# RWKV-7 layer on one core: the recurrence's products and outputs issued in pairs on opposite column tiles, its state sums in pairs with U

## The chip, the core and the metric

The kernel runs on one core of a Trainium2 chip. The metric is the device time in microseconds (us) of one execution. Three runs of the kernel before took 1661.93, 1671.85 and 1673.42 us, so the median is 1671.85. The profiled execution took 1675.05 us, of which 1673.2 us are the span from its first to its last instruction.

The engines are PE (TensorE: matrix products; PEld is its weight load), DVE (VectorE), ACT (ScalarE), POOL (GpSimd) and SP (SyncE, which here only issues DMAs). Each engine runs its own instructions in the order in which they are written, and waits on semaphores for the others.

## The reference

Only layer 0 of the trunk is computed (depth 1), for 2048 tokens, width 1024, 16 heads of 64: an RMS norm, a token shift, projections to r, k, v, gate, decay and a per-channel rate a, a recurrence per head, a group norm, a bonus, a gate and an output projection.

```
dx = token_shift(h) - h;  x_i = h + dx * mu[i]
r, k, v = x_r @ w_r, x_k @ w_k, x_v @ w_v;  g = silu(x_g @ w_g)
decay, a from two small low-rank products;  kk = normalized k * k_k
step(S):  sa = S @ -kk_t
          S = S * decay_t + sa (kk_t * a_t)' + v_t k_t'
          y_t = S @ r_t
y = groupnorm(y) + (r . k . r_k) v;  out = x + (y * g) @ w_out
```

## The kernel before, in words

The program has three stages. Stage one makes the norm, the shifted inputs, and the projections v and gate. Stage two makes, for eight blocks of 256 tokens, the projections k and r and from them the small matrices of the recurrence, which it writes to DRAM; its last block runs the first nine chunks of the recurrence between the pieces of its own work. Stage three runs the other 55 chunks and the output projection. The change touches the last block of stage two and all of stage three.

The recurrence is done in 64 chunks of 32 tokens. A chunk `ch` has two half-steps, `w` = 0 and 1, one for each half of the 16 heads (four pairs `p`, two heads `h` each). A half-step consists of four sets of small float32 products on PE. Each product has 32 output columns and goes to one of four column tiles of 32 (`tile_position`), at 0, 32, 64 or 96:

- **S** (`s_mm`, L255): the products of the chunk's matrix with the state and the values; 8 products, on two column tiles, to `bank[w]`. ACT copies the result (`s_out`, L261) into `misc` or `aux`.
- **U** (`u_mm`, L267): the inverse applied to that copy; 8 products, on two column tiles, to `bank[2]`. ACT copies it into the chunk's `x` (`u_out`, L273).
- **Y** (`y_mm`, L279): the output of the chunk; 8 products, on two column tiles; ACT copies them to `y` on odd chunks (`y_out`, L292).
- **D** (`d_mm`, L300 in the kernel before): the sums for the state; 16 products, on all four column tiles, to `bank[3]`. DVE multiplies them with the decay into the next chunk's `x` (`d_out`, two instructions that the profile has at L52, x<-ubank).

`bank[2]` and `bank[3]` are the two halves of one tile, `ubank` (in stage two `ud`). For one `w`, the chain S, s_out, U, u_out, D, d_out leads from one chunk to the next; the two values of `w` alternate, so Y and D of a half-step belong to the other `w`, half a chunk earlier.

Between these sets the kernel calls `fill`. In stage three `fill` is `after(i)`: first `background(BG)` takes pieces of the group norm, bonus and gating of finished tiles of 128 tokens (`tail`: y instructions on DVE, squares on ACT, a Newton chain on POOL at L405 and L406, transposes on PE at L446) from a list, up to a budget of estimated us per call; a piece `(None, None)` ends a call. Then `fill(F[i % 2])` takes up to that many matmuls of 128x512 of the output projection (`mm`, L486, called dense here) from another list. The amount is multiplied by 1.3, 1 or 0.7, by how many are waiting. The list `work` also takes the columns of a triangular inversion (`inversion`, tiles z and tm on DVE) for two later blocks. PE, DVE, ACT and POOL keep the written order exactly (`manual_schedule`).

Of the kernel before, what the change touches and what calls it, by code (L numbers as in the profile page):

```python
# [24 lines left out]
L = 32  # L25
TB = 256
NC = TB // L
NORM_EPS = 1e-6
F, BG, EV, EV0, GWE, BNE, LOW, SLOW, FAST, INV, INVC = (2, 4), 1.3, (0, 0, 0), (0, 0, 0), 0, 0, 36, 0.7, 1.3, (8, 10), 0.5
LIM = 1.0  # L30
TURN = 1e-9
INL = (0, 0, 3, 3, 3, 0, 0, 0)
# [8 lines left out]
def rwkv7_kernel(ctx, tc, a, T):  # L41
# [209 lines left out]
    def s_mm(ch, w, p):  # L251

        for h in range(2):
            o = col(h, ch + w)
            nc.tensor.matmul(bank[w][o, 1, p], stat[ch % len(stat)][:, h, 4 * w + p, ca], xs[ch % len(xs)][:, h, 4 * w + p],  # L255
                             start=True, stop=True, tile_position=(0, o.start))

    def s_out(ch, w):
        with urgent():
            for h in range(2):  # L260
                nc.scalar.copy(live(w, h)[bu(h)], bank[w][col(h, ch + w), 1])  # L261

    def u_mm(ch, w, p):

        for h in range(2):
            o = col(h, ch)
            nc.tensor.matmul(bank[2][o, p], stat[ch % len(stat)][:, h, 4 * w + p, ca], live(w, h)[:, p], start=True, stop=True,  # L267
                             tile_position=(0, o.start))
# [22 lines left out]
            elif c % 2:  # L291
                nc.scalar.copy(ys[t][:, c // 2, 4 * w : 4 * w + 4], bank[w][:, 0])  # L292

    def d_mm(ch, w):
        if ch + 1 < NCH:
            d, x = dk[ch % len(dk)], xs[ch % len(xs)]
            for p in range(4):
                for h in range(2):
                    for o in (64 * (1 - h), 64 * (1 - h) + L):
                        nc.tensor.matmul(bank[3][o : o + L, p], d[:, h, 4 * w + p, o % 64 : o % 64 + L], x[:, h, 4 * w + p],  # L300
                                         start=True, stop=True, tile_position=(0, o))

    def d_out(ch, w):

# [8 lines left out]
    def chunk(ch, fill):  # L313

        g, c = divmod(ch, NC)
        go = ch != first[0]
        if c == 2 and g + 1 < NB:
            load_g(g + 1)
        for w in range(2):
            for p in range(4):  # L320
                s_mm(ch, w, p)
            s_out(ch, w)
            if w or go:
                end(ch - 1 + w, 1 - w)
            if w == 0:
                if ch + 2 < NCH:
                    load_v(ch + 2)
                if ch + 3 < NCH:
                    load_c(ch + 3)
            fill(2 * w)  # L330
            for p in range(4):
                u_mm(ch, w, p)
            u_out(ch, w)
            fill(2 * w + 1)

    def end(ch, w):

        d_mm(ch, w)
        d_out(ch, w)
        for p in range(4):  # L340
            y_mm(ch, w, p)
        y_out(ch, w)

    dense, evacs, turned, served, al, parts_of = deque(), deque(), set(), [0.0, 0.0], {"low": LOW}, {}
    eng = lambda i: nc.gpsimd if i else nc.vector

    def fill(n):

        served[0] = min(served[0], 6) + n * (FAST if len(dense) > 2 * al["low"] else 1 if len(dense) > al["low"] else SLOW)
        while served[0] > 0 and dense:  # L350
            dense.popleft()[0]()
            served[0] -= 1
# [5 lines left out]
    def tail(t, ks=(0, 1)):  # L358
# [140 lines left out]
        if len(ks) == 1:  # L499
            k = ks[0]  # L500
            out.extend(parts[2 * k] + parts[2 * k + 1] + [(None, None), (0, lambda: (transpose(k), high(k))), (0.7, lambda: rest(k))])
            if k == 0:
                return out, []
            cut = 0
        elif t == 0:

            turns = [[(TURN, lambda k=k: (transpose(k), high(k), rest(k)))] for k in range(2)]
            cut = len(out)
            out.extend(parts[0] + parts[1] + turns[0] + parts[2] + parts[3] + turns[1])
        else:  # L510

            turns = [[(None, None), (0, lambda k=k: (transpose(k), high(k)))] for k in range(2)]
            rests = [[(0.7, lambda k=k: rest(k))] for k in range(2)]
            out.extend(parts[0] + parts[1] + parts[2] + turns[0] + parts[3] + rests[0])
            cut = len(out)
            out.extend([(None, None), (0.0, lambda: None)] + turns[1] + rests[1])
        out.append((0.0, lambda: dense.extend((lambda n=n, ct=ct, k=k: mm(n, ct, k), t)
                                              for n in range(2) for ct in range(NCT) for k in range(3))))
        return out[:cut], out[cut:]
# [697 lines left out]
    with ExitStack() as p1:  # L1217
        def pool(n, bufs, **k):
            return p1.enter_context(tc.tile_pool(name=n, bufs=bufs, reuse_waits="tile", **k))

        c1, yp = pool("c1", 1), pool("yp", 1)
        sps, tps = pool("sps", 1, space=PSUM), pool("tps", 2, space=PSUM)
        for w in range(2):
            bank[w] = sps.tile([P, 2, 4, N], F32, name=f"ybank{w}")
        ud = sps.tile([P, 2, 4, N], F32, name="ubank")
        bank[2], bank[3] = ud[:, 0], ud[:, 1]
        work = deque()
        evs[:] = EV
        al.update(rs=nc.gpsimd, newton=0, wait=2)
        al["sml"] = lambda nm: yp.tile([P, 2, NP], F32, name=nm, tag="sml", bufs=8)  # L1230
        al["sq"] = lambda nm: yp.tile([P, 4, N], F32, name=nm, tag="big", bufs=4)
        al["v"] = lambda nm: yp.tile([P, NP, N], F32, name=nm, tag="v", bufs=4)
        al["o"] = lambda nm: yp.tile([P, NCT, P], F32R, name=nm, tag=nm[:2], bufs=2)
        al["yt"] = lambda nm: tps.tile([P, 4, P], F32, name=nm, tag="tps")
        al["gt"] = lambda nm: yp.tile([P, NP, N], F32, name=nm, tag="gt", bufs=2)
        gb1 = c1.tile([P, 2, 4, N], F32, name="gb")
        nc.sync.dma_start(gb1, a["gn_b"].rearrange("p (i h n) -> p i h n", i=2, n=N))
        al["gb"] = lambda i: gb1[:, i]

        def background(us):  # L1240

            served[1] = min(served[1] + us, us)
            fresh = True
            while evacs or work:
                u, fn = (evacs or work)[0]
                if not fresh and (u is None or u > served[1]):
                    break
                (evacs or work).popleft()
                if u is None:
                    continue  # L1250
                fresh = False
                fn()
                served[1] -= u

        def more_y(t):
            while t > 5 and t - 3 not in turned:
                background(1)
            return yp.tile([P, 2, NP, N], F32, name=f"y{t}", tag="y", bufs=3)

        more[0], first[0] = more_y, NC + 1  # L1260

        with tc.manual_schedule(engines=MANUAL):
            work.extend((0.7, lambda q=q: wo_split(NP - 1, q)) for q in range(2))
            for x in tail(1):
                work.extend(x)
            z = c1.tile([P, L, L], F32, name="z_")
            tm = c1.tile([P, 4 * N], F32, name="tm_")
            inv = deque()
            for g in (NB - 2, NB - 1):
                load, *cols = inversion(g, z, lambda: tm)  # L1270
                inv.extend([(0, load)] + [(None, None), (0, lambda: None)] * 4)
                inv.extend((INVC, x) for x in cols)
            inv_g = inv[L + 6][1]

            inv_last = inv[-1][1]

            def after(i):
                background(BG)
                fill(F[i % 2])

            for ch in range(NC + 1, NCH):
                chunk(ch, after)
                if ch % 4 == 0 and ch > NC:
                    for x in tail(ch // 4 - 1):
                        work.extend(x)
                    for i in range(INV[1] if ch >= INV[0] else 0):
                        if inv:
                            work.append(inv.popleft())
                if ch == NCH - 8:

                    al["low"] = 0
                if ch == NCH - 2:

                    al.update(rs=nc.vector, newton=0.8, wait=0)
                    work.extend(tail(NCH // 4 - 1, (0,))[0])
                if ch == NCH - 2 * NC - 4:
                    assert len(inv) <= L - 1 and not any(x[1] is inv_g for x in work)
                if ch == NCH - NC - 4:
                    assert not inv and not any(x[1] is inv_last for x in work)
            end(NCH - 1, 1)  # L1300
            work.extend(tail(NCH // 4 - 1, (1,))[1])
            while work or dense or evacs:
                background(2)
                fill(6)
# [53 lines left out]
```

## Time and profile before

| | us |
|---|---|
| median of three runs | 1671.85 |
| profiled execution, its own time | 1675.05 |
| its span | 1673.2 |
| stages one and two (0 to 1149) | 1149 |
| stage three, while chunks run (1149 to 1606) | 457 |
| stage three, after the last chunk (1606 to 1673) | 67 |

The profile is of one execution. A group of rows gives an engine, a line of the kernel, an operation, the tiles written and read, and a shape. An idle time is put down to what ended it. The small products of the recurrence are pipelined: a row "x28, 0.58 us" means that 28 of them started and that the last one ended 0.58 us after the first start. A float32 product is two instructions.

### The profile page before, as it was taken

Reading aid. Unit: us, or ns where it says so; the run is one execution under the profiler, and the core shown is the slowest. Engines: PE = TensorE matmul, PEld = TensorE weight load, DVE = VectorE, ACT = ScalarE, POOL = GpSimd, SP = SyncE. Lnnn points to the kernel's source line nnn. Section 1 sums busy time; section 2 is a strip of 40 time slices with the busy share of each in tenths; the row PEclk is TensorE's granted clock in tenths of the full one; section 3 lists DMA queues with packets and bytes.
Section 4 is the critical chain, followed back from the end, with each engine's and each line's share of the span. In section 5 each row is a group of like instructions: output and inputs, shape, how many; then the busy total and the mean of one; then the engine's idle time right before and its main releaser. Section 6 shows DMA issues by size and latency. Waiting matters only on the chain. (4 is left out here: it accounts for less than half of the span.)

```text
span 1673.2 us, 48351 instructions
## 1 busy us (share of the span) xinstructions
PE 1523.3 (91%) x19024; PEld 1257.4 (75%) x19024; DVE 1193.8 (71%) x2917; ACT 762.1 (46%) x1908; POOL 352.8 (21%) x703
## 2 busy tenths in 40 slices
PE   3799999999989999999999997978999998899986
PEld 2578888888878898888888886766666666666765
DVE  7987688676744687979797886666656767766574
ACT  5653233323564545455455544655444444444420
POOL 4500000000012323232222324112222222232220
PEclk9899999999999999999999998989999999999998
DMA  5773334235653556666656578777756577566631
GB/s 180 229 255 140 130 134 147 98 131 170 210 171 87 150 117 156 150 147 165 153 156 149 144 159 213 188 209 190 217 169 176 169 169 194 163 169 181 172 96 47
DMA packets 413409, 269.78 MB, mean 161 GB/s; under 512 B 270048, under 2 KB 345440, under 8 KB 413184
## 3 DMA queue, kind: packets, MB, share of 16 engines
q1 hardware_dynamic: 411840, 262.19, 56.5%
q10 hardware_dynamic: 1344, 4.52, 1.1%
q8 instruction: 150, 2.46, 0.6%
q14 instruction: 75, 0.61, 0.1%
HBM read 159.26 MB, written 111.54 MB: 162 GB/s over the span
## 5 line engine op out<-in xcount | busy, mean ns | idle before, releaser
L52 DVE TENSOR_TENSOR x<-ubank,misc 64x256 f32<-64x256 f32 x216 | 91.1, 422 | 125.2 <-PE ubank L300 121.9
L575 PE MATMUL kps<-mixbl,wkh 128*128 128x256 f32 x448 | 131.7, 294 | 14.8 <-DVE mixbl L187 14.8
L273 ACT COPY x<-ubank 32x256 f32<-32x256 f32 x220 | 79.9, 363 | 128.2 <-PE ubank L267 82.2
L223 POOL MEMSET x<- 32x512 f32 x128 | 66.3, 518 | 328.3 <-PE ybank L279 264.2
L575 PE MATMUL kps<-mixbh,wkh 128*128 128x256 f32 x448 | 135.3, 302 | 0.0
L883 PE MATMUL rps<-mixah,wrh 128*128 128x256 f32 x448 | 133.0, 297 | 2.1 <-ACT sq L61 2.1
L575 PE MATMUL kps<-mixbh,wkl 128*128 128x256 f32 x448 | 130.7, 292 | 0.0
L883 PE MATMUL rps<-mixal,wrh 128*128 128x256 f32 x448 | 127.3, 284 | 0.0
L883 PE MATMUL rps<-mixah,wrl 128*128 128x256 f32 x448 | 127.2, 284 | 0.0
L486 PE MATMUL ops<-woh,oh 128*128 128x512 f32 x256 | 111.6, 436 | 2.4 <-ACT oh L466 2.0
L486 PE MATMUL ops<-woh,ol 128*128 128x512 f32 x256 | 113.3, 443 | 0.0
L486 PE MATMUL ops<-wol,oh 128*128 128x512 f32 x256 | 110.5, 432 | 0.0
L575 PE MATMUL vps<-wvh,mixah 128*128 128x512 f32 x256 | 104.3, 409 | 5.9 <-ACT mixah L97 5.4
L61 ACT ACTIVATE th<-wa,dprm 128x256 f32<-128x256 f32 x64 | 30.3, 474 | 161.1 <-PE wa L835 92.8
L575 PEld LDWEIGHTS kps<-mixbl,wkh 128*128 128x128 f32 x448 | 89.9, 201 | 16.0 <-DVE mixbl L187 16.0
L575 PE MATMUL vps<-wvl,mixah 128*128 128x512 f32 x256 | 101.9, 399 | 0.0
L575 PE MATMUL gps<-wgh,mixbh 128*128 128x512 f32 x256 | 99.9, 390 | 0.0
L575 PE MATMUL gps<-wgl,mixbh 128*128 128x512 f32 x256 | 99.8, 390 | 0.0
L575 PE MATMUL gps<-wgh,mixbl 128*128 128x512 f32 x256 | 99.8, 390 | 0.0
L575 PEld LDWEIGHTS kps<-mixbh,wkh 128*128 128x128 f32 x448 | 89.6, 200 | 9.0 <-issue 9.0
L883 PEld LDWEIGHTS rps<-mixah,wrh 128*128 128x128 f32 x448 | 85.9, 192 | 12.8 <-issue 8.6
L873 POOL TENSOR_TENSOR ra<-th,e 128x256 f32<-128x256 f32 x56 | 47.3, 844 | 218.5 <-issue 149.9
(341 smaller groups left out, 4408.8 us busy)
## 6 DMA issues: line engine op xcount, KB each, us to landing
stat<-sm_d SPq DMA_DIRECT2D x64, 512.0 KB, 4.9
dk<-bt_d SPq DMA_DIRECT2D x128, 128.0 KB, 4.5
sm_d<-ra SPq DMA_DIRECT2D x112, 128.0 KB, 2.6
sm_d<-mo SPq DMA_DIRECT2D x112, 128.0 KB, 2.9
bt_d<-bo SPq DMA_DIRECT2D x56, 256.0 KB, 2.9
up<-up_d SPq DMA_DIRECT2D x66, 128.0 KB, 2.7
xn<-x SPq DMA_DIRECT2D x32, 256.0 KB, 5.2
mkr_d<-mok SPq DMA_DIRECT2D x64, 128.0 KB, 1.7
```

What stands on the lines that cost most here:

```text
L52: return nc.vector.tensor_tensor(out=out, in0=in0, in1=in1, op=op)
L61: nc.scalar.activation(out, in_, f, **k)
L223: nc.gpsimd.memset(x[bu(h), h], 0.0)
L273: (nc.vector.tensor_copy if w and h and evs[0] else nc.scalar.copy)(xs[ch % len(xs)][bu(h), h, 4 * w : 4 * w + 4], bank[2][col(h, ch)])
L486: nc.tensor.matmul(ps, l[:, ct], r(ct, ns), start=(ct == 0 and k == 0), stop=(ct == NCT - 1 and k == 2))
L575: nc.tensor.matmul(ps, x, y, start=first, stop=last)
L873: (nc.vector if b == NB - 1 else nc.gpsimd).tensor_tensor(out=ra[:, :, ca], in0=c3(kn), in1=e[:, :, 0:L], op=mul)
L883: nc.tensor.matmul(ps, x, y, start=first, stop=last)
```

## The change

In a half-step S and Y are now issued in turn, pair by pair, and Y's column tiles are the two that S doesn't use. D and U are issued in turn as well, after three dense matmuls (before: D came straight after S, and U after Y and two dense ones). `F` goes from (2, 4) to (3, 3), the budget `BG` from 1.3 to 1.7 and, in the last four chunks, to 2.4. A forced pause before the second transposes of a tile is taken out, and the inversion's columns join the list in two lots of five in place of one of ten. The first output of stage three has no predecessor as before (`go`).

```diff
--- before.py
+++ after.py
@@ -26,7 +26,7 @@
 TB = 256
 NC = TB // L
 NORM_EPS = 1e-6
-F, BG, EV, EV0, GWE, BNE, LOW, SLOW, FAST, INV, INVC = (2, 4), 1.3, (0, 0, 0), (0, 0, 0), 0, 0, 36, 0.7, 1.3, (8, 10), 0.5
+F, BG, EV, EV0, GWE, BNE, LOW, SLOW, FAST, INV, INVC = (3, 3), (1.7, 2.4), (0, 0, 0), (0, 0, 0), 0, 0, 36, 0.7, 1.3, (8, 10), 0.5
 LIM = 1.0
 TURN = 1e-9
 INL = (0, 0, 3, 3, 3, 0, 0, 0)
@@ -291,14 +291,13 @@
             elif c % 2:
                 nc.scalar.copy(ys[t][:, c // 2, 4 * w : 4 * w + 4], bank[w][:, 0])
 
-    def d_mm(ch, w):
+    def d_mm(ch, w, p):
         if ch + 1 < NCH:
             d, x = dk[ch % len(dk)], xs[ch % len(xs)]
-            for p in range(4):
-                for h in range(2):
-                    for o in (64 * (1 - h), 64 * (1 - h) + L):
-                        nc.tensor.matmul(bank[3][o : o + L, p], d[:, h, 4 * w + p, o % 64 : o % 64 + L], x[:, h, 4 * w + p],
-                                         start=True, stop=True, tile_position=(0, o))
+            for h in range(2):
+                for o in (64 * (1 - h), 64 * (1 - h) + L):
+                    nc.tensor.matmul(bank[3][o : o + L, p], d[:, h, 4 * w + p, o % 64 : o % 64 + L], x[:, h, 4 * w + p],
+                                     start=True, stop=True, tile_position=(0, o))
 
     def d_out(ch, w):
 
@@ -313,33 +312,40 @@
     def chunk(ch, fill):
 
         g, c = divmod(ch, NC)
-        go = ch != first[0]
+        go = ch > max(first[0], 0)
         if c == 2 and g + 1 < NB:
             load_g(g + 1)
         for w in range(2):
+            old = (ch - 1 + w, 1 - w) if w or go else None
             for p in range(4):
                 s_mm(ch, w, p)
+                if old:
+                    y_mm(*old, p)
             s_out(ch, w)
-            if w or go:
-                end(ch - 1 + w, 1 - w)
+            if old:
+                y_out(*old)
+            fill(2 * w)
+            for p in range(4):
+                if old:
+                    d_mm(*old, p)
+                u_mm(ch, w, p)
+            if old:
+                d_out(*old)
+            u_out(ch, w)
             if w == 0:
                 if ch + 2 < NCH:
                     load_v(ch + 2)
                 if ch + 3 < NCH:
                     load_c(ch + 3)
-            fill(2 * w)
-            for p in range(4):
-                u_mm(ch, w, p)
-            u_out(ch, w)
             fill(2 * w + 1)
 
     def end(ch, w):
-
-        d_mm(ch, w)
-        d_out(ch, w)
         for p in range(4):
             y_mm(ch, w, p)
         y_out(ch, w)
+        for p in range(4):
+            d_mm(ch, w, p)
+        d_out(ch, w)
 
     dense, evacs, turned, served, al, parts_of = deque(), deque(), set(), [0.0, 0.0], {"low": LOW}, {}
     eng = lambda i: nc.gpsimd if i else nc.vector
@@ -513,7 +519,7 @@
             rests = [[(0.7, lambda k=k: rest(k))] for k in range(2)]
             out.extend(parts[0] + parts[1] + parts[2] + turns[0] + parts[3] + rests[0])
             cut = len(out)
-            out.extend([(None, None), (0.0, lambda: None)] + turns[1] + rests[1])
+            out.extend(turns[1] + rests[1])
         out.append((0.0, lambda: dense.extend((lambda n=n, ct=ct, k=k: mm(n, ct, k), t)
                                               for n in range(2) for ct in range(NCT) for k in range(3))))
         return out[:cut], out[cut:]
@@ -1275,20 +1281,22 @@
             inv_last = inv[-1][1]
 
             def after(i):
-                background(BG)
+                background(BG[first[0] < 0])
                 fill(F[i % 2])
 
             for ch in range(NC + 1, NCH):
                 chunk(ch, after)
                 if ch % 4 == 0 and ch > NC:
+
                     for x in tail(ch // 4 - 1):
                         work.extend(x)
-                    for i in range(INV[1] if ch >= INV[0] else 0):
-                        if inv:
-                            work.append(inv.popleft())
+                        work.extend(inv.popleft() for i in range(min(len(inv), INV[1] // 2) if ch >= INV[0] else 0))
                 if ch == NCH - 8:
 
                     al["low"] = 0
+                if ch == NCH - 4:
+
+                    first[0] = -1
                 if ch == NCH - 2:
 
                     al.update(rs=nc.vector, newton=0.8, wait=0)
```

**PE, stage three, one half-step and the next.** Before (tile names as the program has them; ubank holds D at L300 and U at L267, ybank S at L255 and Y at L279, ops the dense matmuls):

```order
L255 MATMUL ybank_14828<-x_12870,stat_12863 32x64 x8
L300 MATMUL ubank<-x_12872,dk_12866 32x64 x16
L279 MATMUL ybank_14829<-x_12872,stat_12862 32x64 x8
L486 MATMUL ops_21207<-woh_14283,oh_20878 128x512
L486 MATMUL ops_21207<-wol_14284,oh_20878 128x512
L267 MATMUL ubank<-misc,stat_12863 32x64 x8
L486 MATMUL ops_21207<-woh_14283,ol_20879 128x512
L486 MATMUL ops_21207<-woh_14492,oh_20878 128x512
L486 MATMUL ops_21207<-wol_14493,oh_20878 128x512
L486 MATMUL ops_21207<-woh_14492,ol_20879 128x512
L486 MATMUL ops_21207<-woh_14675,oh_20878 128x512
L486 MATMUL ops_21207<-wol_14676,oh_20878 128x512
```

After (Y is still L279, D is L299, the dense matmuls are L492); the cut begins with the second half of a set of S and Y:

```order
L255 MATMUL ybank_14829<-x_12872,stat_12862 32x64 x2
L279 MATMUL ybank_14828<-x_12872,stat_12862 32x64 x2
L255 MATMUL ybank_14829<-x_12872,stat_12862 32x64 x2
L279 MATMUL ybank_14828<-x_12872,stat_12862 32x64 x2
L492 MATMUL ops_21467<-woh_13457,oh_20779 128x512
L492 MATMUL ops_21467<-wol_13458,oh_20779 128x512
L492 MATMUL ops_21467<-woh_13457,ol_20780 128x512
L299 MATMUL ubank<-x_12872,dk_12866 32x64 x4
L267 MATMUL ubank<-aux,stat_12862 32x64 x2
L299 MATMUL ubank<-x_12872,dk_12866 32x64 x4
L267 MATMUL ubank<-aux,stat_12862 32x64 x2
L299 MATMUL ubank<-x_12872,dk_12866 32x64 x4
```

S and Y alternate by two; three dense matmuls follow; then D and U alternate by four and two. U no longer stands behind Y and two dense matmuls alone, and D no longer ahead of them.

**DVE, stage three, between the start of the Newton chain (written to g) and the first y that reads its end (rst).** x<-ubank,misc x2 is d_out. Before:

```order
L401 TENSOR_REDUCE var_0_20478<-sq_3_20506 128x4
L52 TENSOR_TENSOR x_12870<-ubank,misc 64x256 x2
L58 TENSOR_SCALAR var_0_20478<-var_0_20478 128x16
L58 TENSOR_SCALAR g_0_20557<-var_0_20478 128x16
L52 TENSOR_TENSOR x_12871<-ubank,misc 64x256 x2
L49 SCALAR_TENSOR_TENSOR xr_20339<-ops_20338,xr_20339 128x256
L49 SCALAR_TENSOR_TENSOR xr_20341<-ops_20338,xr_20341 128x256
L52 TENSOR_TENSOR x_12871<-ubank,misc 64x256 x2
L52 TENSOR_TENSOR y_19209<-y_19209,rst_0_20479 128x256
```

After:

```order
L52 TENSOR_TENSOR x_12871<-ubank,misc 64x256 x2
L407 TENSOR_REDUCE var_0_22112<-sq_3_22128 128x4
L58 TENSOR_SCALAR var_0_22112<-var_0_22112 128x16
L58 TENSOR_SCALAR g_0_22172<-var_0_22112 128x16
L52 TENSOR_TENSOR x_12872<-ubank,misc 64x256 x2
L52 TENSOR_TENSOR y_21645<-y_21645,rst_0_22113 128x256
```

Two d_out pairs stood between g and the y instruction, and one stands there now.

**PE, the end of the program: the transposes of the last tile of tokens (yt) and what stands around them.** Before:

```order
L486 MATMUL ops_22579<-woh_14675,oh_22495 128x512
L486 MATMUL ops_22579<-wol_14676,oh_22495 128x512
L486 MATMUL ops_22579<-woh_14675,ol_22496 128x512
L446 MATMUL yt_22626<-consts,y_22030 128x128 x4
L446 MATMUL yt_22675<-consts,y_22030 128x128 x4
L486 MATMUL ops_22682<-woh_13272,oh_22624 128x512
L486 MATMUL ops_22682<-wol_13273,oh_22624 128x512
```

After, where the first set of that tile (yt_22611) is the first row, and that of its second half comes right below the last:

```order
L452 MATMUL yt_22611<-consts,y_22213 128x128 x4
L492 MATMUL ops_22587<-wol_14044,oh_22408 128x512
L492 MATMUL ops_22587<-woh_14043,ol_22409 128x512
L492 MATMUL ops_22587<-woh_14258,oh_22408 128x512
L492 MATMUL ops_22587<-wol_14259,oh_22408 128x512
L492 MATMUL ops_22587<-woh_14258,ol_22409 128x512
L492 MATMUL ops_22587<-woh_14467,oh_22408 128x512
L492 MATMUL ops_22587<-wol_14468,oh_22408 128x512
L492 MATMUL ops_22587<-woh_14467,ol_22409 128x512
L492 MATMUL ops_22587<-woh_14650,oh_22408 128x512
L492 MATMUL ops_22587<-wol_14651,oh_22408 128x512
L492 MATMUL ops_22587<-woh_14650,ol_22409 128x512
```

Both sets stood behind all 48 dense matmuls of the tile ahead; now the first set stands eleven dense matmuls earlier. Over the whole program the dense matmuls behind the last chunk's last product go from 164 to 98, and the transposes there from 24 to 8.

## Rows read from the trace of the kernel before

**Rows 1.** Windows: two stretches; length, busy us (x instructions) of each engine, granted clock, DMA.
```profile
1149.00:1606.00 457.00, 424.10 (x9435) 310.60 (x9434) 294.98 (x747) 213.89 (x576) 122.29 (x302) 0.98 0.63 174
1606.00:1673.00 67.00, 47.66 (x198) 36.60 (x193) 38.73 (x120) 6.37 (x15) 1.40 (x2) 0.87 0.23 73
```

**Rows 2.** Timeline of PE over one half-step: start, us, engine, line, operation, tiles, count.
```profile
1201.29 0.58 PE L255 MATMUL ybank<-x,stat 128*32 128x64 f32 x14
...
1201.74 0.58 PE L300 MATMUL ubank<-x,dk 128*32 128x64 f32 x28
...
1202.15 0.23 PE L300 MATMUL ubank<-x,dk 128*32 128x64 f32 x2
1202.19 0.57 PE L279 MATMUL ybank<-x,stat 128*32 128x64 f32 x14
1202.68 0.50 PE L486 MATMUL ops<-woh,ol 128*128 128x512 f32 x1
...
1203.54 0.64 PE L267 MATMUL ubank<-aux,stat 128*32 128x64 f32 x16
1204.11 0.50 PE L486 MATMUL ops<-wol,oh 128*128 128x512 f32 x1
...
1204.77 0.59 PE L255 MATMUL ybank<-x,stat 128*32 128x64 f32 x14
```

**Rows 3.** Timeline of ACT and DVE in the same half-step.
```profile
1202.03 0.75 ACT L261 COPY aux<-ybank 32x256 f32<-32x256 f32 x2 [0.74 <-PE ybank L255]
1204.21 0.75 ACT L273 COPY x<-ubank 32x256 f32<-32x256 f32 x2 [1.03 <-DVE y L52]
...
1202.53 0.86 DVE L52 TENSOR_TENSOR x<-ubank,misc 64x256 f32<-64x256 f32 x2 [0.82 <-PE ubank L300]
```

**Rows 4.** Who waited for whom: total us, times, longest; 1160 to 1606, the last 1060 to 1152.
```profile
PE ubank L267 <- DVE x L52: 15.1, 36, 1.3
...
PEld ubank L267 <- ACT sq L61: 5.2, 9, 0.8
...
PE ud L267 <- DVE x L52: 14.8, 7, 7.5
```

**Rows 5.** Timeline of POOL: first and last step of one Newton chain, then the bonus product.
```profile
1521.28 0.26 POOL L406 TENSOR_SCALAR var<-var 128x16 f32<-128x16 f32 x1 [9.31 <-DVE g L58]
...
1524.92 0.22 POOL L405 TENSOR_TENSOR rst<-m,g 128x16 f32<-128x16 f32 x1
1525.10 2.04 POOL L384 TENSOR_TENSOR v<-v,misc 128x512 f32<-128x512 f32 x2
```

**Rows 6.** Timeline of PE in a half-step whose two sets of transposes stand together.
```profile
1441.03 0.59 PE L255 MATMUL ybank<-x,stat 128*32 128x64 f32 x14
...
1445.70 0.69 PE L446 MATMUL yt<-consts,y 128*128 128x128 f32 x2 [1.67 <-DVE y L52]
...
1447.17 1.07 PE L267 MATMUL ubank<-aux,stat 128*32 128x64 f32 x16
```

**Rows 7.** Timeline of DVE: the widest inversion step; the last state product of the kernel.
```profile
1449.84 0.41 DVE L52 TENSOR_TENSOR z__14835<-z__14835,tm__14836 128x240 f32<-128x240 f32 x1
...
1598.99 0.86 DVE L52 TENSOR_TENSOR x<-ubank,misc 64x256 f32<-64x256 f32 x2 [0.29 <-PE ubank L300]
```

**Rows 8.** The chain that ended last, its final part: start, us, what.
```profile
1612.65 11.45 PE ops L486 x48
...
1645.09 0.45 PE yt L446 x4
...
1646.18 0.69 DVE ol L52
...
1654.55 0.44 DVE y L52
1655.03 0.70 PE yt L446 x2
...
1656.39 13.14 PE ops L486 x48
```

## The prediction

> **What bounds the kernel now.** I read the windows first [rows 1]. Stage three's chunks take 457 us, in which PE counts as busy for 424 at a granted clock of 0.98, so nearly all at 2.4 GHz. That busy time is records of pipelined products, so I took one half-step apart on PE [rows 2]. S starts at 1201.29, D at about 1201.74, Y at 1202.19 and U at 1203.54, and the next S at 1204.77. The reader should see that D's 32 instructions on four column tiles take about as long as S's or Y's 16 on two: some 0.42 us from first to last start, 0.64 to the last end. A column tile thus takes one instruction in 0.053 us. S and Y each leave two column tiles idle.
>
> Next, what U waits for. s_out ends at 1202.78 [rows 3]. Y ends at 1202.76, and two dense matmuls need 0.59 us (as behind U, from 1204.18 to the next S), so to 1203.35. Yet U starts at 1203.54: d_out ends at 1203.39, and U follows 0.15 us later. The list of waits agrees: PE's U waited for d_out 36 times [rows 4], and some of U's other short idle times have the same end. So a half-step is now 2.25 us from S to U, bounded by D and d_out, then U and the dense matmuls behind it: 0.64 + 0.59 with two, 0.24 more for each further one (48 of them in 11.45 us [rows 8]). With six dense matmuls (two and four) that is 3.95 us.
>
> The rest is in places. Where both sets of transposes stand in one fill, S to U takes 6.14 us and the transposes wait for DVE [rows 6]; the written order has three such places. After the last chunk the windows show 67 us with 47.7 of PE [rows 1], and the chain runs through DVE's group norm of the last tile of tokens: from 1646.18 to the last transposes at 1655.03, when PE has nothing else, then 48 dense matmuls in 13.14 us [rows 8].
>
> **The change, part by part.**
>
> *S with Y.* 32 instructions on four column tiles, as D has today: 0.64 us from start to end, where the two alone cost 0.42 us of starts each.
>
> *D with U.* U's two column tiles take D's eight instructions and U's eight: 16 x 0.053 = 0.85, plus 0.22 for the last, 1.07 us. That merges nothing; but U no longer has d_out ahead of it. U needs s_out: from the end of S 0.10 to the copy's start and 0.75 for the two copies [rows 3], then 0.15, so 1.00 us after S and Y end. The three dense matmuls take 0.83 (0.59 + 0.24), so the first D goes ahead and hides 0.1. D and U end 1.00 + 1.07 - 0.10 = 1.96 us (rounded) after S and Y.
>
> *The new wait.* The next S now has d_out straight ahead, and U and three dense matmuls cover it. D's last product ends about 0.1 us before U's; 0.15 later d_out starts, takes 0.86 [rows 3], and 0.15 after that S starts: 1.05 us after U, against 0.83 of dense work. Behind S waits Y, and it needs u_out, 0.03 + 0.75 + 0.15 = 0.93 us after U: hidden by the same 1.05. A regular half-step is then 0.64 + 1.96 + 1.05 = **3.65 us** with six dense matmuls; 109 of them lie between stage three's first S and its last d_out, 398 us.
>
> *Extras on PE, from the order.* 27 sets of four transposes (about 0.4 us; 0.45 in [rows 8]) stand behind S and Y (8 times) or behind D and U (19 times), partly in the 0.2 us that PE waits anyway; and 14 half-steps have a fourth dense matmul ahead of U. Together 11 us.
>
> *DVE.* d_out is in DVE's queue behind what `background` put there in both fills. Between one d_out's end and the next one's start 0.15 + 0.64 + 1.96 + 0.04 = 2.79 us are free. With 0.44 us for a y instruction [rows 8] and up to 0.41 for an inversion step [rows 7], 32 of the 104 gaps in the order hold more, by 16 us in sum, 1.9 at most. I take 15. The Newton chain on POOL takes 3.9 us from g to rst (1521.28 to 1525.14), the bonus 1.0 per instruction behind it [rows 5]; with one d_out less between g and the y instruction DVE comes about 0.3 us too early once per tile of 128 tokens: 4 us in 13.
>
> *Odds.* Single late copies cost U 5.2 us now, behind ACT's squares [rows 4]; with a late load or two I leave 6 us.
>
> Sum to the last d_out: 398 + 11 + 15 + 4 + 6 = 434 us. Before, it ended at 1599.85 [rows 7], 451 us after stage three's chunks began at 1149 [rows 1]. **Gain 17 us.** The three places of [rows 6] are in that difference.
>
> *The end.* Counted from the last d_out: S and Y are done at 0.8, four transposes and four dense matmuls follow, U ends at 2.9, u_out stands behind a cast and two squares on ACT until 4.05, Y ends at 4.85. Then 39 dense matmuls at 0.24, to 14.1; transposes and their cast, and eleven dense matmuls meanwhile; ol on DVE ends at 16.1. From there the second half's chain: 1646.87 to 1655.03 today, so 8.2 less ol's overlap, and two xr of 0.38: last transposes at 23.5. Then 0.7 + 0.6, the 48 dense matmuls as today at 13.14, and 3.7 from their end to the span's end: 41.6 us. Before: 1673.2 - 1599.85 = 73.4. **Gain 31 us**, one tile's norm and dense work having moved into the chunks, whose sums above hold them.
>
> *Last block of stage two.* 18 half-steps save up to 0.42 us each where PE sets the pace (7.6), and U's 14.8 us of waits on d_out [rows 4] may go or turn into waits of S. But d_out now stands behind the DVE work of the fill ahead. No row prices that; I bound it by a gain of 15 and a loss of 8, and take a gain of 4, as the rows nearest are those of S and Y in stage three with most of the rest hidden.
>
> *Queues.* The loads for later chunks are issued one set of products later, but two to three chunks (15 us and more) ahead of use: nothing. The removed pause costs nothing by itself: its transposes stand one fill behind the gating they need.
>
> Sum: 17 + 31 + 4 = 52 us off the profiled 1675, so 1623 for a like run; that run was 3.2 above the median, hence **1620 us**.
>
> **Rivals.**
>
> *S and Y don't overlap.* If products of two banks and two `x` tiles didn't run side by side, each half-step would keep 0.42 us: 109 x 0.42 = 46 at most, some 38 where DVE is late anyway, so 1658 us. Against it stands D, with 28 starts in 0.36 us, one in 13 ns, from two halves of `x` [rows 2], and a few D and S instructions of different banks already overlap at their border. The Trainium skill, "TensorE: Matmul & The Clock Gate", part 1 ("Wait — 56ns, not 53.3ns?"), says that start-to-start never drops below about 25 ns however few columns; by it 32 instructions need 0.80 us and S with Y would gain nothing, which is this rival. The 13 ns of [rows 2] contradict it. 8%.
>
> *Slower: DVE sets the pace.* The budget rises by 30% while the time for it shrinks, and now S itself waits behind DVE. I count 19 us of lateness (0.17 us per half-step). If real DVE and POOL work with their own waits (ol on a cast, y on rst and v) made d_out late by 1.0 us on average, the chunks would take 109 x 4.65 + 17 = 524 us, 73 more than now, and with the 35 gained elsewhere the whole 1710 us. From 0.65 us on the gains elsewhere are gone, from 0.8 on it is slower by over 1%. For it: U was already waiting for DVE in both stages [rows 4]. Against it: DVE was busy for 295 of 457 us [rows 1], and gets some 20 more. 5%.
>
> *More gain.* Stage two yields its 15 us and DVE's lateness overlaps with PE's extras: 1595 us, at a chance of 12%.
>
> **Numbers.** The forecast and its neighbourhood (1600 to 1650) has 75%. The range 1594 to 1652 takes in the bounds of stage two (+12, -11), of DVE's lateness (0 to 35) and the better case, and leaves out the two worse rivals. About 1% (17 us) is what a measurement can tell from no change: faster 0.88 (the forecast and more gain), within 1% 0.08 (the first rival and the second where it is mild), slower 0.04.
>
> **What would show it.** Right: S and Y in one row group of about 0.64 us; S starting 0.15 us after d_out in most half-steps of about 3.65 us; no half-step of 8 us; a stretch of some 42 us behind the last d_out, with 48 dense matmuls at its end. Wrong: S and Y lasting 1 us; DVE's d_out with no idle time ahead of it in most half-steps; U waiting for ACT well beyond 1.0 us; or a stage two that ends later than at 1149.

## The result: slower, 1712.1 us against 1669.3

The changed kernel takes 1712.1 us (median of four, 1708.9 to 1713.8), the one before 1669.3; the ratio is 1.0256 (95%: 1.0234 to 1.0279). The forecast was 1620, with a range up to 1652. The profiled execution took 1713.7, its span is 1711.6. By its windows (columns as in [rows 1]):

```profile
1149.50:1668.00 518.50, 475.84 (x9446) 318.82 (x9447) 326.24 (x786) 214.75 (x577) 128.65 (x316) 0.98 0.54 157
1668.00:1711.60 43.60, 31.62 (x181) 23.99 (x181) 20.47 (x68) 5.82 (x15) 0.00 (x0) 0.88 0.17 54
```

Stage three begins where it did, with its first S at 1149.5 (before: 1149.2). Its chunks last 518 us to the end of the last d_out, where 434 were forecast and 451 was the time before. The stretch behind lasts 43.7 us, where 41.6 were forecast and 73.4 was the time before. So 84 of the 91 us by which the span misses the forecast lie in the half-steps. One of them, with three and three dense matmuls, on PE, ACT and DVE:

```profile
1197.39 0.32 PE L299 MATMUL ubank<-x,dk 128*32 128x64 f32 x8
...
1198.20 0.29 PE L267 MATMUL ubank<-misc,stat 128*32 128x64 f32 x4
...
1199.33 0.52 PE L255 MATMUL ybank<-x,stat 128*32 128x64 f32 x4
1200.01 0.63 PE L279 MATMUL ybank<-x,stat 128*32 128x64 f32 x3 [0.17 <-ACT x L273]
...
1200.72 0.31 PE L279 MATMUL ybank<-x,stat 128*32 128x64 f32 x3
...
1199.60 0.75 ACT L273 COPY x<-ubank 32x256 f32<-32x256 f32 x2 [1.87 <-DVE x L52]
...
1198.61 0.88 DVE L52 TENSOR_TENSOR x<-ubank,misc 64x256 f32<-64x256 f32 x2 [0.80 <-PE ubank L267]
```

D starts at 1197.39 and U's last product ends at 1198.49: 1.10 us for both (forecast: 1.07). d_out follows at 1198.61 and ends at 1199.49. Then comes what the forecast did not have: u_out, whose products are done at 1198.49 too, starts only at 1199.60, 0.11 us after d_out's end. So Y's products run from 1200.01 to 1201.03, though S had started at 1199.33, and S with Y lasts 1.70 us instead of 0.64. In the row of u_out the releaser is d_out. It is so throughout: over 109 half-steps u_out starts 0.09 to 0.11 us after d_out's end (first to last tenth), at the median 1.10 us after U's end. The list of waits, 1190 to 1650 (total us, times, longest):

```profile
ACT x L273 <- DVE x L52: 165.0, 78, 5.0
...
PEld ybank L279 <- ACT x L273: 51.3, 188, 0.6
ACT x L273 <- POOL x L223: 38.4, 19, 2.3
...
PEld ybank L255 <- DVE x L52: 15.6, 47, 0.5
```

ACT's u_out waited for d_out, and Y's weight loads waited for u_out 188 times. (The 165 us are all of ACT's idle time ahead of these copies, also the part before U was done.) In 19 cases the list names POOL's zeroing of an `x` tile instead; there, too, u_out starts 0.11 us after d_out's end. None of this stands in [rows 4], where the one that waits for d_out is U on PE. S itself waits little: d_out is two instructions, and S's first product needs only the first.

The chain at the end of the program (start, us, what) answers to [rows 8]:

```profile
1673.15 9.11 PE ops L492 x39
1682.26 0.45 PE yt L452 x4
...
1683.36 0.69 DVE ol L52
...
1692.78 0.70 PE yt L452 x2
...
1694.14 13.30 PE ops L492 x48
```

Here the order of things is as forecast: 39 dense matmuls behind the last chunk, the second half's norm from 1682 to 1693, and 48 dense matmuls at the end.

### The profile page after: what moved, and what is told of

It reads as the page before. It is cut to its first block, busy times and chain, and to the rows that moved or that the text cites. A ratio compares the mean times of both kernels' runs of the same rounds, so it can differ in the third digit from the quotient of the medians.

```text
span 1711.6 us, 48221 instructions
## 1 busy us (share of the span) xinstructions
PE 1566.9 (92%) x19024; PEld 1253.1 (73%) x19024; DVE 1206.6 (70%) x2904; ACT 762.2 (45%) x1908; POOL 357.9 (21%) x716
## 4 chain that ended last, share of the span: by engine, by line
PE 50%; DVE 22%; ACT 8%; issue 6%; DMA 5%; POOL 3%; SPq 1%; DVEq 0%; ACTq 0%; POOLq 0%
PE gps L581 9%; PE vps L581 8%; PE kps L581 8%; PE rps L889 5%; PE ops L492 5%; DVE x L52 4%; ACT x L273 4%; PE ubank L299 3%; PE ybank L279 2%; PE lps L643 2%; DVE z L52 2%; PE mps L925 2%; DVE tm L52 2%; DVE y L52 2%; DMA xn<-x 1%
## 5 line engine op out<-in xcount | busy, mean ns | idle before, releaser
L255 PE MATMUL ybank<-x,stat 128*32 128x64 f32 x1760 | 111.6, 226 | 19.1 <-DVE x L52 8.9
L279 PE MATMUL ybank<-x,stat 128*32 128x64 f32 x1760 | 103.2, 225 | 23.3 <-ACT x L273 6.9
L299 PEld LDWEIGHTS ubank<-x,dk 128*32 128x32 f32 x3456 | 91.4, 110 | 40.7 <-issue 37.8
L255 PEld LDWEIGHTS ybank<-x,stat 128*32 128x32 f32 x1760 | 67.6, 110 | 70.8 <-issue 45.7
L492 PE MATMUL ops<-woh,oh 128*128 128x512 f32 x256 | 113.6, 444 | 1.1 <-ACT oh L472 0.7
L492 PE MATMUL ops<-woh,ol 128*128 128x512 f32 x256 | 112.3, 439 | 0.0
L299 PE MATMUL ubank<-x,dk 128*32 128x64 f32 x3456 | 110.6, 229 | 0.1
L279 PEld LDWEIGHTS ybank<-x,stat 128*32 128x32 f32 x1760 | 67.7, 110 | 57.3 <-ACT x L273 57.3
L492 PE MATMUL ops<-wol,oh 128*128 128x512 f32 x256 | 107.1, 418 | 0.0
```

Source lines behind the costliest of these rows:

```text
L279: nc.tensor.matmul(bank[w][o, 0, p], stat[ch % len(stat)][:, h, 4 * w + p, cr], xs[ch % len(xs)][:, h, 4 * w + p], start=True, stop=True, ...
L492: nc.tensor.matmul(ps, l[:, ct], r(ct, ns), start=(ct == 0 and k == 0), stop=(ct == NCT - 1 and k == 2))
```

## The experiments

The theories: **A**, u_out waits for d_out because ACT and DVE would read the same PSUM bank (`ubank`: U in one half, D in the other), and the program lets one engine at a time read it, in the order in which the two are written. **B**, the wait is about the state tile `x`, which both write. **C**, the forecast's rival: the greater background budget makes DVE late. Where each profiled run's time lies (us: first S of stage three; from there to the last d_out's end; from there to the span's end), with the medians and the ratios to the kernel before that ran on the same chip:

| kernel | to stage three | chunks | end | median | ratio (95%) |
|---|---|---|---|---|---|
| before | 1149.2 | 450.6 | 73.4 | 1669.3 | |
| changed | 1149.5 | 518.4 | 43.7 | 1712.1 | 1.0256 (1.0234 to 1.0279) |
| e1 changed, U in another bank | 1133.7 | 469.7 | 42.2 | 1648.6 | 0.9889 (0.9855 to 0.9922) |
| e2 before, U in another bank | 1140.0 | 426.0 | 72.0 | 1639.6 | 0.9837 (0.9797 to 0.9876) |
| e3 changed, u_out first | 1138.4 | 505.3 | 42.5 | 1688.2, one run | |
| e4 changed, old budget | 1149.1 | 509.1 | 70.6 | 1730.8 | 1.0376 (1.0340 to 1.0412) |
| e5 e1 with four pauses | 1135.0 | 433.6 | 44.9 | 1613.7 | 0.9661 (0.9637 to 0.9686) |
| e6 e1, bonus first | 1134.5 | 463.1 | 42.1 | 1643.1 | 0.9851 (0.9823 to 0.9879) |
| e7 e2 with the new budget | 1138.4 | 439.4 | 41.5 | 1620.7 | 0.9713 (0.9697 to 0.9730) |
| e8 before, new budget | 1144.5 | 474.1 | 41.2 | 1657.2 | 0.9938 (0.9915 to 0.9961) |
| e9 e7 with four pauses | 1140.2 | 427.7 | 43.2 | 1613.2 | 0.9675 (0.9648 to 0.9701) |
| e10 e5, bonus first | 1131.2 | 435.6 | 44.5 | 1618.3 | 0.9695 (0.9669 to 0.9720) |
| e11 e1 with the old budget | 1133.1 | 420.0 | 71.9 | 1626.8 | 0.9746 (0.9718 to 0.9773) |

### e1: U's products in another bank

```diff
-            nc.tensor.matmul(bank[2][o, p], stat[...][:, h, 4 * w + p, ca], live(w, h)[:, p], ...
+            nc.tensor.matmul(bank[w][o, 1, p], stat[...][:, h, 4 * w + p, ca], live(w, h)[:, p], ...
...
-                    xs[ch % len(xs)][bu(h), h, 4 * w : 4 * w + 4], bank[2][col(h, ch)])
+                    xs[ch % len(xs)][bu(h), h, 4 * w : 4 * w + 4], bank[w][col(h, ch), 1])
```

> The changed kernel with one edit: U's products go to the half of bank[w] that S leaves free once s_out has copied it, instead of the PSUM bank that D writes. Theory A (one bank): in the changed kernel u_out on ACT starts 0.10 us after the end of d_out on DVE in every half-step, because both read the same PSUM bank and the program keeps their order; Y waits for u_out. With U elsewhere u_out should start 0.1 us after U's end, beside d_out; S to S of a half-step with three and three dense matmuls falls from 4.68 us to between 3.7 and 3.9, 109 of them, and the time from 1712 to between 1605 and 1640. Theory B (both write the state tile x, and the wait is about x): u_out still starts 0.10 us behind d_out, and the time stays at 1705 to 1718. Theory C (the greater budget of background work makes DVE late): nothing changes, 1705 to 1718, with d_out as late as before the edit.

1648.6 us: 64 less than the changed kernel, by this edit alone. The same engines in one half-step:

```profile
1195.58 0.29 PE L267 MATMUL ybank<-aux,stat 128*32 128x64 f32 x4
...
1196.70 0.32 PE L255 MATMUL ybank<-x,stat 128*32 128x64 f32 x3
1196.81 0.25 PE L279 MATMUL ybank<-x,stat 128*32 128x64 f32 x2
...
1195.92 0.75 ACT L273 COPY x<-ybank 32x256 f32<-32x256 f32 x2 [0.92 <-PE ybank L267]
...
1195.83 0.88 DVE L52 TENSOR_TENSOR x<-ubank,misc 64x256 f32<-64x256 f32 x2
```

U ends at 1195.87, u_out starts at 1195.92, beside d_out at 1195.83, and Y stands interleaved with S from 1196.81 on. In three of four half-steps u_out now starts 0.05 to 0.11 us after U (1.10 at the median before the edit). The wait itself is gone from the program: of the 110 u_outs of stage three, the first copy has a wait for a semaphore of DVE in 108 cases in the changed kernel, and in none in e1. S and Y take 0.66 us where nothing holds them (0.77 at the median), and a half-step with three and three dense matmuls 3.93 us instead of 4.69 (medians; A had 3.7 to 3.9). B and C fall as causes of these 64 us: the tile `x` and the budget are the same. The edit moves U to another bank and to another tile at once; which of the two the program's wait goes by, no run separates. But the time is 9 us above what A had expected, and 36 us are missing in the chunks against the forecast's 434. They lie mostly in single half-steps of 5 to 6 us, one or two per tile of 128 tokens:

```profile
1345.02 0.40 PE L492 MATMUL ops<-wol,oh 128*128 128x512 f32 x1
1347.69 0.60 PE L255 MATMUL ybank<-x,stat 128*32 128x64 f32 x3 [2.27 <-DVE x L52]
...
1343.20 1.25 DVE L52 TENSOR_TENSOR y<-y,rst 128x256 f32<-128x256 f32 x1 [1.35 <-POOL rst L411]
1344.49 1.15 DVE L438 TENSOR_TENSOR y<-y,aux 128x256 f32<-128x256 f32 x1
...
1347.12 0.88 DVE L52 TENSOR_TENSOR x<-ubank,misc 64x256 f32<-64x256 f32 x2
...
1342.95 0.22 POOL L411 TENSOR_TENSOR rst<-m,g 128x16 f32<-128x16 f32 x1
1343.13 2.23 POOL L390 TENSOR_TENSOR v<-v,misc 128x512 f32<-128x512 f32 x2
```

PE's last dense matmul ends at 1345.42, and S waits until 1347.69 for d_out, which starts at 1347.12: ahead of it in DVE's queue the norm's first product waited for rst until 1343.20, then took 1.25 us, and the second 1.15, while POOL's bonus products ran (1343.13 to 1345.36); three more of 0.42 follow. Elsewhere the first two take 0.42 as well. In stage three e1 has 17.4 us of waits for rst (14 times) and 23.0 us of such excess (30 products).

### e2: the same edit in the kernel before

The diff is that of e1.

> The kernel before with the same single edit: U's products in bank[w] and not in D's bank. Theory A: U on PE no longer waits for d_out; PE's waits of U on d_out (15.1 us in stage three, 14.8 in stage two's last block) go, U starts when Y and two dense matmuls are done, 0.19 us earlier in a regular half-step, and the time falls by 10 to 30 us to between 1640 and 1660. If that wait was covered by others (s_out, the dense matmuls): 1665 to 1675. Theory C has no say here, since the budget is the old one.

1639.6 us, just under the range: 28 less than before. A half-step with two and four dense matmuls falls from 3.95 to 3.75 us, the 0.2 expected, and no wait of U for d_out is left among the waits. This edit alone, without the change, is worth more than the change with it (e1).

### e3: u_out ahead of d_out

```diff
+            u_out(ch, w)
             if old:
                 d_out(*old)
-            u_out(ch, w)
```

> The changed kernel with u_out written ahead of d_out, U and D still in one bank. Theory A: the order in the text sets which of the two waits. u_out starts 0.1 us after U, and d_out 0.1 us after the end of u_out; now S waits (0.1 + 0.75 + 0.1 + 0.43 = 1.4 us after U instead of 0.82) and Y no longer does (S and Y together about 1.1 us instead of 1.70). The sum stays about the same: 1695 to 1725. Theory B: d_out waits for u_out only in the half-steps in which both write the same x (every second one); 1660 to 1690. Theory C: u_out starts early and d_out does not move; Y's wait goes: 1620 to 1650.

One run: 1688.2. On ACT and then on DVE in the same half-step:

```profile
1199.71 0.75 ACT L273 COPY x<-ubank 32x256 f32<-32x256 f32 x2 [0.66 <-PE ubank L267]
...
1200.49 0.88 DVE L52 TENSOR_TENSOR x<-ubank,misc 64x256 f32<-64x256 f32 x2 [0.60 <-ACT x L273]
```

Now d_out waits for u_out's end, throughout (at the median it starts 0.99 us after D, and in nine of ten half-steps at least 0.95 after it). S starts 1.37 us after U and S with Y takes 1.10, as A expected. The total is 7 us under A's range; stage three begins 11 us earlier, which A's sum had not in it. It lies in the range that B gave, but B wanted this wait in every second half-step alone, and it is in both kinds (1.00 and 0.95 us). So the order in the text chooses which of the two readers waits.

### e4: the old budget

```diff
-... (3, 3), (1.7, 2.4), ...
+... (3, 3), (1.3, 1.3), ...
...
-            out.extend(turns[1] + rests[1])
+            out.extend([(None, None), (0.0, lambda: None)] + turns[1] + rests[1])
```

> The changed kernel with the background budget of the kernel before (1.3 throughout) and with its pause between the two halves' transposes; the new order of products and the three and three dense matmuls stay. Theory A: u_out still starts 0.10 us behind d_out, and a regular half-step stays at 4.5 to 4.7 us; fewer late d_outs give back up to 15 us in the chunks, and the work that is now left for the end costs 20 to 35: 1705 to 1745. Theory C: d_out is on time again, and the chunks shrink from 518 us to about 440: 1640 to 1670.

1730.8 us: with less work on DVE the kernel is slower still, as A said. The chunks give back 9 us, the longer end takes 27, and the wait is there (1190 to 1640):

```profile
ACT x L273 <- DVE x L52: 135.8, 65, 5.7
```

### e5 and e6: what the norm does on DVE

e5 is e1 with `wait=4` instead of 2, in `al.update(rs=nc.gpsimd, newton=0, wait=2)`.

> e1 with one edit: four pauses of a fill instead of two between the Newton chain on POOL and the group norm's first product on DVE. Theory A with a second cause: what e1 still lacks (chunks of 470 us against the 434 forecast) is one stall per tile of 128 tokens, in which the norm's first products wait on DVE for rst (17.4 us in 14 waits), and then take 1.25 and 1.15 us instead of 0.42 beside POOL's bonus products, with d_out and so S behind them (S 3.1 us after U instead of 0.83). Two fills later both are over: the stalls go, 12 to 13 tiles by 2.3 us, so chunks of 437 to 447 us and 1612 to 1628 us in all. Rival (DVE just has too much background work, wherever it stands): the stalls come back at another place, 1635 to 1655.

1613.7 us, in A's range. POOL's chain and bonus, and the norm's first products on DVE:

```profile
1311.73 0.22 POOL L411 TENSOR_TENSOR rst<-m,g 128x16 f32<-128x16 f32 x1
1311.91 2.04 POOL L390 TENSOR_TENSOR v<-v,misc 128x512 f32<-128x512 f32 x2
...
1315.73 0.41 DVE L52 TENSOR_TENSOR y<-y,rst 128x256 f32<-128x256 f32 x1
1316.17 0.43 DVE L438 TENSOR_TENSOR y<-y,aux 128x256 f32<-128x256 f32 x1
```

Here the norm begins 3.8 us after rst is done, and 1.8 after the bonus products; in e1 it began 0.03 us after rst in every tile. No wait for rst is left, and 2 slow products instead of 30. The chunks last 433.6 us, and a half-step with three and three dense matmuls 3.63 (in the chunks A had expected 437 to 447).

In e6 the two bonus products stand ahead of the Newton chain instead:

```diff
+        for k in ks:
+            out.append((0.1, lambda k=k: scale_bonus(k)))
+
         @step(0.4)
         def _():
             st["rg"], st["rm"] = sml("g"), sml("m")
...
-        for k in ks:
-            out.append((0.1, lambda k=k: scale_bonus(k)))
```

> e1 with one edit: POOL's two bonus products of a tile stand ahead of its Newton chain instead of behind it, so that they no longer run beside the norm's first two products on DVE. If the 1.25 and 1.15 us are due to running beside POOL: both go back to 0.42 to 0.45 us, 13 tiles by 1.5 us are saved, less what rst comes later (up to 2.2 us per tile where POOL is not done when g comes): 1625 to 1655, and in the trace no slow y product beside a bonus product; other DVE work beside the bonus is slowed instead if it is of the same kind. If they are slow for another reason: still 1.25 and 1.15 us.

1643.1 us. Of DVE, and of POOL's bonus:

```profile
1339.24 0.40 DVE L407 TENSOR_REDUCE var<-sq 128x4 f32<-128x256 f32 x1
1339.68 0.58 DVE L58 TENSOR_SCALAR var<-var 128x16 f32<-128x16 f32 x1
1340.29 0.97 DVE L58 TENSOR_SCALAR g<-var 128x16 int32<-128x16 int32 x1
...
1345.25 0.43 DVE L52 TENSOR_TENSOR y<-y,rst 128x256 f32<-128x256 f32 x1 [2.49 <-POOL rst L411]
1345.71 0.42 DVE L439 TENSOR_TENSOR y<-y,aux 128x256 f32<-128x256 f32 x1
...
1339.18 2.05 POOL L390 TENSOR_TENSOR v<-v,misc 128x512 f32<-128x512 f32 x2
```

Both products have 0.43 and 0.42 us now, so it was the bonus beside them. What now stands beside it are the two small steps of the variance (0.58 and 0.97 us instead of 0.17), while the reduction keeps its 0.40. But the Newton chain starts later, and the waits for rst grow from 17.4 to 38.1 us, so little is won. The Trainium skill, "SBUF — State Buffer", section "SBUF: two separate sides", says that of a DVE operation with two SBUF inputs and a GpSimd operation that reads SBUF the second waits for the whole of the first. The rows fit this in the main: in the tile of e1 shown above each y product ended 0.28 us after the bonus product beside it, where alone it takes 0.42.

### e7, e8, e9 and e11: which half of the change is worth what

e8 is the kernel before with the new budget, the split inversion steps and no pause, two and four dense matmuls as before; e7 is e8 with the edit of e1; e9 is e7 with `wait=4`; e11 is e1 with the edit of e4 (as in e4, the inversion steps stay split).

> e2 (the order of products of the kernel before, U in the other bank) with the background budget of the changed kernel, its inversion steps and no pause between the two halves' transposes; two and four dense matmuls, S and Y one after the other, D ahead of Y as before. Theory A: the order by pairs of products buys 0.2 to 0.3 us per half-step over e2's 3.8 to 3.9, and the earlier norm the shorter end; this kernel has the second without the first: chunks of 430 to 450 us and an end of 42 to 46 us, 1605 to 1635. If the shorter end came from the order of products: 1635 to 1660.

> The kernel before with the background budget alone (1.7 and 2.4, inversion steps by halves, no pause), U and D in one bank, everything else as before. Theory A: in the old order U waits for d_out, u_out has nothing left to wait for; d_out comes later by the greater budget, which costs 0.1 to 0.3 us per half-step, and the end shortens by 25 to 30 us: 1645 to 1675. Theory C (the budget is what made the changed kernel slow): 1690 to 1730.

> e7 (order of products of the kernel before, U in the other bank, budget of the changed kernel) with the four pauses of e5. Theory A, second cause: the waits for rst (27.6 us in 13) and the slow y products go, and what is left of late d_outs; a half-step with two and four dense matmuls has 3.75 us there against 3.63 with three and three in e5, so if both orders are free of late d_outs this one is 109 x 0.12 = 13 us slower than e5, 1618 to 1630. If the old order bears a late d_out better, because S, D and Y are 2 us of products behind it and only S waits (in e5 S waits straight behind d_out): 1598 to 1612, and the order by pairs has no worth of its own.

> e1 (order by pairs, U in the other bank) with the background budget and the pause of the kernel before, as in e4. It is e2 with the new order of products and three and three dense matmuls alone. Theory A: with little background work on DVE, d_out is on time, a half-step with three and three dense matmuls is 3.63 us as in e5, chunks of 415 to 430 us, the long end of 70 to 72: 1625 to 1640, the same as e2 (1639.6) or up to 13 faster. If the order by pairs itself makes S late behind d_out: 1640 to 1655.

Medians in us ("new order" has three and three dense matmuls, "old order" two and four):

| | old order of products | new order |
|---|---|---|
| one bank, old budget | 1669.3 | 1730.8 (e4) |
| one bank, new budget | 1657.2 (e8) | 1712.1 (changed) |
| other bank, old budget | 1639.6 (e2) | 1626.8 (e11) |
| other bank, new budget | 1620.7 (e7) | 1648.6 (e1) |
| other bank, new budget, four pauses | 1613.2 (e9) | 1613.7 (e5) |

All three of e7, e8 and e11 fell in A's ranges, and C falls as the cause of the slowdown: the new budget gains 11 us with the old order (e8, against 1668.1 for the kernel before, measured beside it). But DVE's lateness has a price of its own. The new budget lengthens the chunks in every pair: by 23 us (e8), 13 (e7 against e2), 9 (changed against e4) and 50 (e1 against e11), and shortens the end by 27 to 32. So once U has its own bank, the greater budget makes the new order 22 us slower, until the pauses of e5. With one bank the new order costs 55 to 62 us, whatever the budget. With its own bank for U it gains 13 with the old budget, loses 28 with the new, and is worth nothing beside the four pauses. Its regular half-step is shorter (3.63 against 3.75 us), but S stands right behind d_out in it. S's waits for d_out, e5 (1150 to 1565):

```profile
PEld ybank L255 <- DVE x L52: 21.9, 48, 2.4
...
PE ybank L255 <- DVE x L52: 11.1, 15, 1.9
```

and e9:

```profile
PE ybank L255 <- DVE x L52: 1.7, 2, 1.5
PEld ybank L255 <- DVE x L52: 1.7, 6, 0.4
```

In the old order Y, U and six dense matmuls stand between d_out's products and the next S, so a late d_out rarely reaches S, though it starts no earlier there (0.52 us after D on average in e9, 0.40 in e5); the mean half-step is 3.92 us in e9 and 3.98 in e5. e9 lay between its two expectations, nearer to the second.

### e10: both edits

The diff is that of e5 and e6 together.

> e5 with POOL's bonus products ahead of the Newton chain, as in e6. In e5 no y product runs beside a bonus product and none waits for rst, so there is nothing left for it to give: 1608 to 1618, the same as e5 within 0.3%; a wait for rst that comes back would show as 1618 to 1630.

1618.3 us, 0.3 above the range for "the same"; its interval overlaps with that of e5. So nothing was won. The best kernels, e5 and e9, beat both given ones: U in a bank of its own, the new budget and four pauses, in either order of products.

## Why the prediction was wrong

- **The step that failed** is in "The new wait": Y "needs u_out, 0.03 + 0.75 + 0.15 = 0.93 us after U: hidden". It let u_out start when U is done. It starts when d_out is done. From U's end to u_out's end 1.10 + 0.75 us passed, and S with Y took 1.70 us instead of 0.64. Part of these 1.06 us covers what the sum had counted apart (late d_outs, S's own wait), so that the mean half-step grew by 0.77 us, from 434/109 = 3.98 to 4.76. That d_out and u_out read one bank was to be seen beforehand: the prediction had from [rows 4] that U on PE waits for d_out, which reads the other half of that bank, and did not ask what this means for the second reader. In [rows 3] u_out's releaser is an instruction of DVE, though u_out takes only what PE wrote. (The row names a y product, which has nothing to do with u_out and is only the last that DVE had finished; that u_out has a wait for DVE at all was the sign, in 98 of 110 u_outs of stage three.) Before, this wait was over before U had begun (d_out ended at 1203.39, U started at 1203.54); putting D and U side by side made it the longest of the half-step. e1 takes it away and e3 turns it round. The Trainium skill, "PSUM — Partial Sum Buffer", section "PSUM bank collisions raise a hardware error", says that the compiler back end's scheduler makes any two instructions of different engines that touch the same bank and 32 partitions depend on each other, two readers too. The runs agree: u_out starts 0.09 to 0.11 us behind d_out with one bank and 0.05 to 0.11 us behind U with two.
- **A second step was too small.** The Newton chain was put at 4 us and DVE's lateness at 15. From e1 to e5 the chunks lose 36 us by two more pauses: waits for rst and products slowed beside POOL's bonus. The prediction saw the one as 0.3 us per tile and did not see the other, though the new distance (one d_out less between g and y) is what put the two side by side: 12 slow products in stage three before, 30 after. In the changed kernel the waits for rst were 5.5 us in 13, near the 4 forecast, and the slow products came to 23; most of it was hidden behind the first wait, for the old budget gives back 9 us of chunks there (e4) and 50 with U in another bank (e11).
- **Right**: S with Y on four column tiles (0.66 us in e1), D with U (1.10 for 1.07), the D and U group ending 1.92 us after S and Y (0.82 + 1.10; forecast 1.96), the end (43.7 for 41.6). In the sum for the end, 16.1 + 8.2 + 0.76 make 25.1, and no row gives the 1.6 us that were taken off to get 23.5; the last transposes began 24.9 us after the last d_out. With both causes removed, e5's half-step is 3.63 us (3.65 forecast), its chunks 433.6 (434), its time 1613.7 (1620). The time agrees partly by chance: stage three begins 10 us ahead of the forecast's 1145, and the end is 3 us longer. The forecast described a kernel whose U has a bank of its own and whose norm comes two fills later.
- **Stage two**: a gain of 4 was taken from bounds of +15 and -8. It was 0 in the changed kernel and 15.8 in e1: the same wait held it.
- **The rivals**: "DVE sets the pace" named 1710 us, but by another mechanism. It wanted d_out late by 1.0 us on average; d_out started 0.24 us after D at the median (0.42 on average, where 0.15 is none), and e4 and e8 go against it. "S and Y don't overlap" is refuted by e1's 0.66 us. The 4% for "slower" was too low, because the only slower case considered was one of DVE's load. And the sign "S and Y lasting 1 us" did come, but from u_out's wait, not from the rival that it was meant for.
- **The sum**: 1149.5 + 518.4 + 43.7 against 1145 + 434 + 41.6: 84 us of the miss are the chunks, 6.6 the rest. e1 and e5 take 66 and 32 us off the span, 98 in all, and end 7 us below the forecast's 1620.6 for the span.

## What to carry to other kernels

Before two products are put side by side, ask for each bank who reads it, with which engine, and in what order: here two readers of one bank took turns, because the program has a wait between them, and the second one's consumer paid for the first. A wait that costs nothing because it is over early is still in the program, and an edit that brings its two ends together makes it the path; look for releasers in the trace that have no data for the waiting instruction. And moving a chain closer to its consumer (here Newton's) can also bring two engines together that slow each other.

## What the hardware showed unexpectedly

- DVE's 128x256 products took 1.25 and 1.15 us beside POOL's products and 0.42 without; steps of 0.17 us took 0.58 and 0.97; the reduction (0.40, e6) and d_out, which reads PSUM, were not slowed (0.43 for each of its instructions that ran beside a bonus product in e5).
- The 16 products (32 instructions) of S and Y on four column tiles, from two banks and two state tiles, run in 0.66 us to the last end in e1, as D's 32 from one bank did before (0.64).
